# A fixed order for weight sums, loads and roundings at the turn into a two-layer MLP on one core

## The chip, the cores and the metric

The kernel runs on one core of one Trainium2 chip. The metric is device time in microseconds (us). Before the change the median of three runs is 742.66 us (740.46 to 743.09).

A core has five instruction queues that run beside each other and wait for one another through semaphores: TensorE (PE, matrix products), VectorE (DVE), ScalarE (ACT), GpSimd (POOL) and SyncE (SP, which here only issues transfers). Each executes its own instructions in the order in which the program lists them. [...]

## The reference

One block of a language model on 512 tokens with 1024 features, all in float32: an RMS norm, one wide projection, a gated linear attention branch and a softmax attention branch that are merged, an output projection with a residual, and then the part that the change touches.

```python
h = h + merged @ w_out[l]                                          # 1024 x 1024
m = rmsnorm(h, g_mlp[l])
h = h + jnp.square(jax.nn.relu(m @ w_ff1[l])) @ w_ff2[l]           # 1024 x 4096, 4096 x 1024
return rmsnorm(h, g_final)
```

## The kernel before

**Precision.** TensorE multiplies a rounded format (fp32r). To keep float32 accuracy every operand is kept as a rounded part `h` (high, one ScalarE copy that rounds) and a remainder `l` (low, one VectorE subtraction of the rounded part from the original), and each product is three matmuls (`mm3`, lines 88 to 90): high x high, high x low, low x high.

**Seven products instead of eight.** The output projection and each quarter of the MLP cut their operands into 2 x 2 blocks and form the result from seven block products, after Strassen and Winograd. They are numbered 1 to 7. Some of them need a sum of weight blocks. Blocks are called B11, B12, B21, B22; each lies in two tiles, the halves g = 0 and g = 1, of 128 x 1024 numbers (512 KB).

**Phases.** `Mlp(n)` is one phase. There are four quarters; a quarter has a first phase (f0, f1, f2, f3: `m @ w_ff1`) and a second one (g0 to g3: `@ w_ff2`). A first phase runs its products in the order 1, 2, 5, 6, 7, 4, 3. In f0 product 1 reads the weight block in tile B11 as loaded, product 2 reads B21, product 5 reads B11 after **sum 1** (B12 added from memory), product 6 reads B11 after **sum 2** (B22 added as well), product 4 reads B11 after **sum 4** (B21 added), product 7 reads B12 after **sum 3** (B22 added), and product 3 reads B22. So tile B11 goes through a fixed sequence: round (`hi`, line 1616), remainder (`lo`, line 1620), add the next block (`sum`, line 1626), round again. In f0 and in all second phases a sum is an accumulating transfer on GpSimd's queue; in f1 to f3 it is a VectorE addition (line 1628). `load` (line 1606) issues a plain transfer on SP. A second phase keeps its B11 in the tile that w_out's B21 and its last sum used, its B21 where the first phase had B21, and its B12 in the first phase's B12 tile.

**The tokens' side.** `flipped(i)` transposes 128 token rows on TensorE; rows 0 and 1 feed one half of the token blocks, rows 2 and 3 the other. `m_copy` (line 1503) copies the flipped blocks out of the accumulators with the norm's gain, `m_sum` (line 1521) forms sums of token blocks, `m_hi` (line 1508) and `m_lo` (line 1512) round and subtract. `sink` takes a product out of the accumulators.

**The turn.** Before f0 stands the output projection, whose products 1, 2, 5, 6, 3, 7, 4 are traced one by one with everything between them. Rows get their norm as soon as they are complete: `first_half_square` and `second_half_square` (line 174) sum squares on ScalarE, `row_rstd` (lines 181 and 184) makes the row factor on VectorE and GpSimd, `scaled` (lines 1479 and 1480) or, for rows 2 and 3, the last loop of the turn (line 1865) multiplies the row by it.

**What sets the order.** From `begun` on, which is before the output projection's second product, TensorE, ScalarE and VectorE keep the order in which the program is traced (`in_program_order`), and GpSimd keeps it too. The turn is written out statement by statement. After it, every instruction of f0 to g3 is a step with a due time in a table, in units of 10 ns; the steps are sorted by these times and traced in that order. f0 has its own table, `F0_PLACES`; a quarter starts at `base = FLIPS + q * PERIOD`, a first-phase product takes 16 x 36 units and a second-phase product 8 x 22.77 x 3. The times give the order only: an instruction runs as soon as its engine has reached it and its semaphores are there. SP's transfers have no such chain of order of their own.

In the turn as it stands, in f0's order of work: sum 3 is issued after the roundings for w_out's product 4, then come the roundings of f0's B11 and sum 1, the squares and the token copies; product 5's weights are rounded from the step table (540 and 640), after product 2's (340 and 440).

Of the kernel before, what the change touches and what calls it, by code (L numbers as in the profile page):

```python
# [22 lines left out]
KD = D // P  # L23
# [33 lines left out]
def tile_block(ctx: ExitStack, tc: tile.TileContext, t, out: bass.AP):  # L57
# [122 lines left out]
    def row_rstd(parts):  # L180
        nc.vector.scalar_tensor_tensor(
            parts[:, 3:4], parts[:, 1:2], 1.0 / D, parts[:, 2:3], op0=ALU.mult, op1=ALU.add
        )
        nc.gpsimd.tensor_tensor(parts[:, 3:4], parts[:, 3:4], mhalf, op=ALU.pow)
        return parts[:, 3:4]
# [746 lines left out]
    NP = 4  # L932
# [419 lines left out]
    def wo_product(m, rbs=range(2), ps_=range(NP)):  # L1352
        accs = wo_accs.get(m) or wo_accs[1]
        for p in ps_:
            lh, ll = wo_left[p][m]
            wh, wl = wo_right[m][p // 2]
            for rb in rbs:
                tok = slice(rb * P, (rb + 1) * P)
                mm3(accs[rb], lh[:, tok], ll[:, tok], wh[:, p % 2, :], wl[:, p % 2, :],
                    m in (1, 2, 5) and p == 0, p == NP - 1, m not in (1, 2, 5))  # L1360
# [102 lines left out]
    def add_rows(i, c, acc, op=ALU.add):  # L1463
        hc = hrow[i][:, c * S : (c + 1) * S]
        nc.vector.tensor_tensor(hc, hc, acc, op=op)  # L1465
# [8 lines left out]
    def second_half_square(i, c):  # L1474
        square_half(hrow[i], c, hparts[i], ms_rows[i], False)

    def scaled(i, rs):
        m = ms_rows[i]
        nc.vector.tensor_scalar(m[:, 0:S], hrow[i][:, 0:S], rs, None, op0=ALU.mult)
        nc.scalar.activation(m[:, S:D], hrow[i][:, S:D], AF.Copy, scale=rs)  # L1480
# [13 lines left out]
    def m_copy(x, half, ks, by_vector=False):  # L1494
        if x not in m_raw:
            m_raw[x] = pair_tiles(f"mr{x}")
        for k in ks:
            src, gain = fm.block(half, k)
            dst = m_raw[x][k % NP // 2][:, k % 2]
            if by_vector:  # L1500
                nc.vector.tensor_scalar(dst, src, gain, None, op0=ALU.mult)
            else:
                nc.scalar.activation(dst, src, AF.Copy, scale=gain)

    def m_hi(m, b):
        if m not in m_left:
            m_left[m] = quarter(f"mh{m}"), quarter(f"ml{m}")
        nc.scalar.activation(m_left[m][0][:, 2 * b : 2 * b + 2], m_raw[m][b], AF.Copy)
# [72 lines left out]
    class Mlp:  # L1581
# [27 lines left out]
            return self.tiles(self.RIGHT.get(m, B11))  # L1609

        def hi(self, m, g):
            if (self.n, m) == (0, 5):
                self.right[m, g] = [u4(f"{self.name}{m}{g}{x}") for x in "hl"]
            else:
                self.right[m, g] = halves(2, S, f"{self.name}{m}{g}")
            nc.scalar.activation(self.right[m, g][0], self.tile_of(m)[g], AF.Copy)
# [205 lines left out]
    for rb in range(2):  # L1822
        wo_product(3, (rb,))
        add_rows(rb, 1, zs_[rb])
        second_half_square(rb, 1)
        scaled(rb, row_rstd(hparts[rb]))
    wo_product(7, (0,))
    add_rows(2, 1, xs_[0], ALU.subtract)
    wo_right[4] = [split_part(B21, 0, "bo4")]
    wo_right[4].append(split_part(B21, 1, "bo4"))  # L1830
    phases[1].load(B11)
    for g in range(2):
        f0.sum(3, g)
    flipped(0)
    for g in range(2):
        f0.hi(1, g)
    f0.lo(1, 0)
    f0.sum(1, 0)
    first_half_square(2, 1)
    wo_product(7, (1,), range(2))  # L1840
    flipped(1)
    wo_product(7, (1,), range(2, NP))
    add_rows(3, 1, xs_[1], ALU.subtract)
    f0.lo(1, 1)
    f0.sum(1, 1)
    m_copy(1, 0, range(NP))
    for b in range(2):
        m_hi(1, b)
        m_lo(1, b)
    first_half_square(3, 1)  # L1850
    m_copy(2, 0, range(NP, KD))
    for b in range(2):
        m_hi(2, b)
    wo_product(4, (0,))
    add_rows(2, 0, xs_[0])
    wo_product(4, (1,))
    add_rows(3, 0, xs_[1])
    for b in range(2):
        m_lo(2, b)
    second_half_square(2, 0)  # L1860
    rs2 = row_rstd(hparts[2])
    second_half_square(3, 0)
    rs3 = row_rstd(hparts[3])
    for i, r in ((2, rs2), (3, rs3)):
        nc.vector.tensor_scalar(ms_rows[i], hrow[i], r, None, op0=ALU.mult)
    FIRST, SECOND, PERIOD = 36, 22.77, 7857

    steps = []

    def step(at, what, *args):  # L1870
        steps.append((at, len(steps), what, args))
# [17 lines left out]
    for at, ks in ((800, range(2)), (801, range(2, NP))):  # L1889
# [3 lines left out]
    step_pairs(0, {5: (1060, 1115), 6: (1460, 1515), 7: (2055, 2110), 4: (2550, 2600), 3: (3345, 3400)}, m_hi)  # L1893
    step_pairs(0, {5: (1165, 1230), 6: (1540, 1600), 7: (2150, 2260), 4: (2610, 2670), 3: (3480, 3540)}, m_lo)
    F0_PLACES = {
# [6 lines left out]
            4: PLACES["F sink"][4], 3: PLACES["F sink"][3],  # L1902
        },
        "G load": {B21: (1800, 1900), B12: (2240, 2350), B22: (3380, 3500)},
    }
    for m in (4, 3):
        F0_PLACES["F sink"][m] = tuple(x + FLIPS for x in F0_PLACES["F sink"][m])
    for q in range(NQ):
        base, f, g = FLIPS + q * PERIOD, phases[2 * q], phases[2 * q + 1]
        for name, ph in (("F", f), ("G", g)):  # L1910
            at = base
            for m in ph.order:
                if ph.last and m == 4:
                    break
                step_product(at + (7 * slot if ph.second else 0) - (FLIPS if ph is f0 and m == 1 else 0), ph, m)
                at += 8 * SECOND * 3 if ph.second else slot
            for kind in ("hi", "lo", "sum", "load", "sink"):
                kind_of = f"{name} {kind}"
                if q == 0 and kind_of in F0_PLACES:
                    step_pairs(0, F0_PLACES[kind_of], getattr(ph, kind))  # L1920
                    continue
                places = PLACES[kind_of]
                if ph.last and kind == "sink":
                    places = {m: at for m, at in places.items() if m != 4}
                step_pairs(base, places, getattr(ph, kind))
        for kind in ("relu", "square", "left sum", "left hi", "left lo"):
            step_pairs(base, PLACES[kind], getattr(f, kind.replace(" ", "_")))
# [4 lines left out]
        step(base + (7000, 7001, 7250, 7450)[i], out_first, i)  # L1932
    for i in range(2):
        step(base + 7080 + i, out_square, i, slice(0, S))
        step(base + 7180 + i, out_rstd, i)
        step(base + 7440 + 2 * i, out_left, i)
        step(base + 7300 + i, out_right, i)
        step(base + 7441 + 2 * i, out_store, i)
    for _, _, what, args in sorted(steps, key=lambda x: x[:2]):
        what(*args)  # L1940
    in_program_order(begun, PE_ONLY + SPLITTERS)
    in_program_order(attending, (mybir.EngineType.Pool,))
    last_rows(g3)

# [27 lines left out]
```

## Time and profile before

| what | us |
|---|---|
| median of three runs | 742.66 |
| the three runs | 743.09, 742.66, 740.46 |
| the profiled execution, its own time | 743.55 |
| its span | 741.9 |
| TensorE busy | 728.0 (98%) |
| VectorE busy | 626.1 (84%) |
| ScalarE busy | 494.2 (67%) |
| GpSimd busy | 219.4 (30%) |

All times in the views below are from the start of the span of that one execution. A busy TensorE is not a TensorE at its peak: its matmuls are pipelined, and how fast it goes is read from the starts of its matmuls. A name such as `f0x<-mh,f060h` reads: into accumulator f0x, from the tokens' rounded part and from the rounded part of f0's product 6, half 0. `w<-in_w_ff` is a transfer of MLP weights into one of the block tiles: on SP a load, on POOL a sum. In the chain of waits each line is a start, a length and what ran or was waited for. A view of stretches gives the stretch, its length, and for each engine its busy time and number of instructions, then the granted TensorE clock as a share, the busy share of the transfer engines and GB/s. In the list of waits the numbers are the sum, how often, and the longest.

### The profile page before, as it was taken

The page shows a single profiled execution, that of the slowest core. Times are in us where ns is not written, and L with a number is a line of the kernel's source. Part 1 is how long each engine was busy: PE and PEld are TensorE (multiplying, and loading weights), DVE is VectorE, ACT ScalarE, POOL GpSimd, SP SyncE. Part 2 cuts the span into 40 slices and gives each one's busy share as a digit, 9 for nine tenths or more (in the row PEclk, how much of TensorE's full clock was granted, in tenths as well). Part 3 has the DMA queues.
Part 4 walks back from the last instruction along what each step waited for, and adds up shares of the span by engine and source line. Part 5 has one row for each costly group of instructions (what it writes and reads, how often), then busy time and mean ns, then how long its engine had stood idle before and what let it go on. Part 6 is the DMA issues. An engine that isn't in the chain of part 4 may idle for free.

```text
span 741.9 us, 11474 instructions
## 1 busy us (share of the span) xinstructions
PE 728.0 (98%) x4226; PEld 643.0 (87%) x4226; DVE 626.1 (84%) x861; ACT 494.2 (67%) x809; POOL 219.4 (30%) x284
## 2 busy tenths in 40 slices
PE   9999999999999999999999999999999999999995
PEld 7888888888888888899888988889988998899984
DVE  7777887889998788798898879998699869987896
ACT  7557575586596675888856869544774477537764
POOL 0732020242754633146752312200211012101215
PEclk9999999999999999999999999999999999999998
DMA  9849682521221333458988979751987088816763
GB/s 312 270 108 215 215 178 86 89 55 28 64 57 53 50 83 97 111 130 215 270 163 229 229 153 216 191 153 59 245 183 196 15 239 180 196 53 149 167 111 114
DMA packets 80520, 109.95 MB, mean 148 GB/s; under 512 B 15920, under 2 KB 34352, under 8 KB 80464
## 3 DMA queue, kind: packets, MB, share of 16 engines
q1 hardware_dynamic: 63088, 75.64, 32.5%
q0 software_dynamic: 17088, 33.30, 26.6%
q8 instruction: 33, 0.54, 0.3%
q10 hardware_dynamic: 288, 0.28, 0.1%
q14 instruction: 23, 0.19, 0.1%
HBM read 104.22 MB, written 2.10 MB: 143 GB/s over the span
## 4 chain that ended last, share of the span: by engine, by line
PE 84%; DVE 6%; DMA 4%; issue 3%; POOL 1%; ACT 1%; POOLq 0%; DVEq 0%; ACTq 0%
DMA w<-in_w_ff 4%; PE first L326 3%; PE tp L1122 2%; PE zb L88 1%; PE zb L90 1%; PE zb L89 1%; DVE h L1465 1%; PE f1x L89 1%; PE f3x L90 1%; PE f1x L90 1%; PE f2x L90 1%; PE f2x L89 1%; PE f3x L89 1%; PE f3x L88 1%; PE f2x L88 1%
## 5 line engine op out<-in xcount | busy, mean ns | idle before, releaser
L1626 POOL DMA_DIRECT2D w<-in_w_ff x40 | 48.3, 1219 | 260.4 <-DMA w<-in_w_ff 137.1
L1102 DVE TENSOR_REDUCE top<-s 128x1 f32<-128x512 f32 x32 | 21.6, 682 | 4.9 <-PE s L90 4.8
L1107 ACT ACTIVATE e<-s,top 128x512 f32<-128x512 f32 x32 | 22.0, 687 | 3.5 <-DVE top L1102 2.5
L94 DVE TENSOR_TENSOR pT<-tp,pT 128x512 fp32r<-128x512 f32 x32 | 21.8, 683 | 2.4 <-ACT pT L93 1.9
L93 ACT ACTIVATE pT<-tp 128x512 fp32r<-128x512 f32 x32 | 19.1, 596 | 3.2 <-PE tp L1122 3.2
L1122 PE MATMUL tp<-ident,e 128*128 128x128 f32 x128 | 19.5, 274 | 0.0
L88 PE MATMUL av<-pT,v 128*128 128x256 f32 x64 | 19.1, 299 | 0.0
L90 PE MATMUL av<-pT,v 128*128 128x256 f32 x64 | 18.2, 285 | 0.0
L89 PE MATMUL av<-pT,v 128*128 128x256 f32 x64 | 18.1, 284 | 0.0
L1122 PEld LDWEIGHTS tp<-ident,e 128*128 128x128 f32 x128 | 15.2, 140 | 3.1 <-ACT e L1113 0.7
L94 POOL TENSOR_TENSOR qF<-qk,qF 128x512 fp32r<-128x512 f32 x4 | 6.6, 1642 | 37.6 <-ACT qF L93 37.6
L667 POOL DMA_DIRECT2D gvw<-in_w_in x4 | 4.8, 1230 | 38.7 <-DVE gvw L672 34.0
L667 POOL DMA_DIRECT2D zaw<-in_w_in x4 | 4.9, 1228 | 32.7 <-DVE zaw L672 28.0
L1628 DVE TENSOR_TENSOR w<-w,w 128x1024 f32<-128x1024 f32 x12 | 14.4, 1220 | 0.1
L980 POOL DMA_DIRECT2D w<-in_w_out x10 | 12.2, 1400 | 6.5 <-DVE bo60l L94 5.3
L88 PE MATMUL s<-kbuf,q 96*128 96x512 f32 x32 | 14.1, 439 | 0.0
L1153 POOL TENSOR_TENSOR mx<-tb,yg 128x256 f32<-128x256 f32 x8 | 7.7, 964 | 19.8 <-DVE tb L1150 13.9
L577 ACT ACTIVATE bds<-bd 128x512 f32<-128x512 f32 x4 | 2.4, 597 | 15.8 <-PE bd L555 15.8
L89 PE MATMUL s<-kbuf,q 96*128 96x512 f32 x32 | 12.6, 395 | 0.0
L90 PE MATMUL s<-kbuf,q 96*128 96x512 f32 x32 | 12.6, 393 | 0.0
L1113 ACT ACTIVATE e<-e,tot 128x512 f32<-128x512 f32 x16 | 11.6, 726 | 1.3 <-DVE tot L1112 1.3
L89 PEld LDWEIGHTS av<-pT,v 128*128 128x128 f32 x64 | 12.2, 190 | 0.3
(2155 smaller groups left out, 3249.6 us busy)
## 6 DMA issues: line engine op xcount, KB each, us to landing
w<-in_w_ff SPq DMA_DIRECT2D x48, 512.0 KB, 5.5
w<-in_w_ff POOLq DMA_DIRECT2D x40, 512.0 KB, 6.2
w<-in_w_out POOLq DMA_DIRECT2D x10, 512.0 KB, 8.8
grw<-in_w_in SPq DMA_DIRECT2D x8, 512.0 KB, 8.6
zaw<-in_w_in SPq DMA_DIRECT2D x8, 512.0 KB, 7.3
gvw<-in_w_in SPq DMA_DIRECT2D x8, 512.0 KB, 5.0
w<-in_w_out SPq DMA_DIRECT2D x16, 256.0 KB, 5.5
w220f<-in_w_ff SPq DMA_DIRECT2D x8, 512.0 KB, 6.0
```

The lines of the kernel that those rows point to most:

```text
L88: nc.tensor.matmul(acc, lh, rh, start=start, stop=False, skip_group_check=onto)
L89: nc.tensor.matmul(acc, lh, rl, start=False, stop=False, skip_group_check=onto)
L90: nc.tensor.matmul(acc, ll, rh, start=False, stop=stop, skip_group_check=onto)
L93: nc.scalar.activation(hi, src, AF.Copy)
L94: rest.tensor_tensor(lo, src, raw(hi), op=ALU.subtract)
L326: nc.tensor.matmul(f_accs[i], a[:, i * P : (i + 1) * P], b, start=k == 0 and x == 0, stop=k == KD - 1 and x == 2)
L980: nc.gpsimd.dma_start(d, rows.rearrange("(k t p) w -> p t k w", t=2, p=P)[:, x // 2], accum_op=ALU.add)
L1102: nc.vector.tensor_reduce(top, acc, axis=AX.X, op=ALU.max, negate=True)
L1107: nc.scalar.activation(e, acc, AF.Exp, bias=top, accum_out=tot[:, qt % 2 : qt % 2 + 1])
L1122: nc.tensor.transpose(tp[:, k * P : (k + 1) * P], e[:, k * P : (k + 1) * P], ident)
L1626: nc.gpsimd.dma_start(d, self.source(src, g), accum_op=ALU.add)
L1628: nc.vector.tensor_tensor(d, d, self.tiles(src)[g], op=ALU.add)
```

## The change

- The rounding of f0's B11 (`f0.hi(1, ...)`) moves up, between the squares of rows 0 and 1, and with it the remainders and sum 1, ahead of w_out's product 7.
- Sum 3 and the load of g0's B11 leave that place. Sum 3 comes behind sum 2; the load becomes a step (2250 and 2260).
- The rounding, remainder and sum 2 for product 5 move from the step table into the turn, around w_out's product 4, ahead of product 2's rounding, which moves into the turn too. Product 5's rounded weights now lie in the shared `wh`/`wl` buffers, and product 1's in buffers of their own.
- In the step table product 6's second rounding, the remainders and sum 4 get earlier times; the load of g0's B12 and B22 and g0's sum 3 get other times; f1's load of B11 moves from 2802 and 2988 to 6680 and 6690.
- In the last group the row factors of rows 0 and 1 (`out_rstd`) go from 7180 to 7235, which is behind the last weight remainder (7231).
- SP's transfers among the steps are chained in the traced order.

```diff
         def hi(self, m, g):
-            if (self.n, m) == (0, 5):
+            if (self.n, m) == (0, 1):
                 self.right[m, g] = [u4(f"{self.name}{m}{g}{x}") for x in "hl"]
...
         second_half_square(rb, 1)
+        f0.hi(1, rb)
+        if rb == 1:
+            f0.lo(1, 0)
         scaled(rb, row_rstd(hparts[rb]))
+    f0.sum(1, 0)
+    f0.lo(1, 1)
+    f0.sum(1, 1)
     wo_product(7, (0,))
     add_rows(2, 1, xs_[0], ALU.subtract)
     wo_right[4] = [split_part(B21, 0, "bo4")]
     wo_right[4].append(split_part(B21, 1, "bo4"))
-    phases[1].load(B11)
-    for g in range(2):
-        f0.sum(3, g)
     flipped(0)
-    for g in range(2):
-        f0.hi(1, g)
-    f0.lo(1, 0)
-    f0.sum(1, 0)
     first_half_square(2, 1)
...
     add_rows(3, 1, xs_[1], ALU.subtract)
-    f0.lo(1, 1)
-    f0.sum(1, 1)
     m_copy(1, 0, range(NP))
     for b in range(2):
         m_hi(1, b)
         m_lo(1, b)
     first_half_square(3, 1)
-    m_copy(2, 0, range(NP, KD))
-    for b in range(2):
-        m_hi(2, b)
     wo_product(4, (0,))
     add_rows(2, 0, xs_[0])
+    f0.hi(5, 0)
+    f0.lo(5, 0)
+    f0.sum(2, 0)
     wo_product(4, (1,))
     add_rows(3, 0, xs_[1])
-    for b in range(2):
-        m_lo(2, b)
     second_half_square(2, 0)
     rs2 = row_rstd(hparts[2])
     second_half_square(3, 0)
     rs3 = row_rstd(hparts[3])
+    f0.hi(5, 1)
+    f0.lo(5, 1)
+    f0.sum(2, 1)
+    m_copy(2, 0, range(NP, KD))
+    for x in range(2):
+        f0.hi(2, x)
+        m_hi(2, x)
+        f0.sum(3, x)
     for i, r in ((2, rs2), (3, rs3)):
         nc.vector.tensor_scalar(ms_rows[i], hrow[i], r, None, op0=ALU.mult)
+    for x in range(2):
+        f0.lo(2, x)
+        m_lo(2, x)
...
-        "F hi": {2: (340, 440), 5: (540, 640), 6: (1450, 1760), 7: (1985, 2090), 4: (2610, 2710), 3: (3140, 3240)},
-        "F lo": {2: (580, 690), 5: (810, 990), 6: (1640, 1870), 7: (2110, 2225), 4: (2730, 2845), 3: (3250, 3365)},
-        "F sum": {2: (930, 1110), 4: (1760, 1990)},
+        "F hi": {6: (1390, 1520), 7: (1985, 2090), 4: (2610, 2710), 3: (3140, 3240)},
+        "F lo": {6: (1640, 1760), 7: (2110, 2225), 4: (2730, 2845), 3: (3250, 3365)},
+        "F sum": {4: (1650, 1770)},
...
-            1: (1280, 1290), 2: (1310, 1745), 5: (1780, 1975), 6: (2300, 2555), 7: (2860, 3130),
+            1: (1280, 1290), 2: (1310, 1880), 5: (1780, 1975), 6: (2300, 2555), 7: (2860, 3130),
...
-        "G load": {B21: (1800, 1900), B12: (2240, 2350), B22: (3380, 3500)},
+        "G load": {B21: (1800, 1810), B12: (2240, 2270), B11: (2250, 2260), B22: (3400, 3510)},
+        "G sum": {**PLACES["G sum"], 3: (3000, 3100)},
...
+    for m in (1, 2, 4):
+        F0_PLACES["G sum"][m] = tuple(x + FLIPS for x in F0_PLACES["G sum"][m])
...
+                if q == 1 and kind_of == "F load":
+                    places = {**places, B11: (6680 - base, 6690 - base)}
...
-        step(base + 7180 + i, out_rstd, i)
+        step(base + 7235 + i, out_rstd, i)
...
+    stepped = traced()
     for _, _, what, args in sorted(steps, key=lambda x: x[:2]):
         what(*args)
     in_program_order(begun, PE_ONLY + SPLITTERS)
+    in_program_order(stepped, SP_ONLY)
     in_program_order(attending, (mybir.EngineType.Pool,))
```

## The prediction

> **What bounds the kernel now.** I read the page first, then the chain of waits, and then cut the turn into the MLP into stretches, one product of the first group (f0) after another. The page has TensorE busy 98% of the span, so the time can only fall where TensorE stands still, and only the turn and the last microseconds offer that. The view of busy time by stretches, cut where the first matmul of a product starts (product 1, the two late flips, then products 2, 5, 6, 7, 4, 3; columns: stretch, length, then busy time and count of TensorE, its weight loads, VectorE, ScalarE, GpSimd):
>
> ```profile
> 412.13:417.89 5.76, 5.76 (x50) 5.75 (x49) 4.55 (x9) 5.28 (x12) 1.37 (x3) 1.00 1.07 247
> 417.89:419.55 1.66, 1.66 (x18) 1.66 (x17) 1.66 (x3) 0.90 (x1) 0.00 (x0) 1.00 1.16 210
> 419.55:425.38 5.83, 5.83 (x51) 5.83 (x50) 3.64 (x5) 4.53 (x11) 1.38 (x2) 1.00 0.87 234
> 425.38:431.76 6.38, 6.08 (x50) 5.86 (x49) 4.42 (x8) 4.12 (x7) 1.06 (x1) 1.00 0.72 119
> 431.76:439.46 7.70, 6.26 (x51) 5.85 (x49) 7.70 (x10) 6.56 (x11) 2.41 (x2) 1.00 0.59 86
> 439.46:447.18 7.72, 5.92 (x51) 5.75 (x49) 4.23 (x6) 4.29 (x7) 2.03 (x2) 1.00 0.92 262
> 447.18:453.01 5.83, 5.83 (x49) 5.83 (x50) 5.65 (x8) 5.83 (x10) 0.41 (x1) 1.00 0.99 206
> 453.01:458.77 5.76, 5.76 (x51) 5.76 (x50) 4.68 (x7) 5.40 (x9) 1.20 (x1) 1.00 1.04 276
> ```
>
> Seven products do the same work. The undisturbed ones take 5.76, and the flips 1.66. So the group needs 7 x 5.76 + 1.66 = 41.98 us and takes 46.64: **4.66 us are stall**, 0.62 in product 5, 1.94 in product 6, and 1.96 at the end of product 7, where product 4 should begin; 0.14 lies in the rest. The granted clock is 1.00 in every stretch. The chain of waits says who is late (start, length, what):
>
> ```profile
> 407.41 1.23 DVE f010l L1620
> ...
> 408.93 7.56 DMA w<-in_w_ff
> ...
> 420.98 7.75 DMA w<-in_w_ff
> ...
> 428.75 1.06 ACT f060h L1616
> ...
> 435.14 8.89 DMA w<-in_w_ff
> ...
> 444.12 1.07 ACT f041h L1616
> ...
> 447.18 0.36 PE f0x L88
> ```
>
> This is a ladder: a remainder frees block B11, an accumulating transfer adds the next block onto it (sum 1, then sum 2, then sum 4), the result is rounded for products 5, 6, 4, and its remainder lets the next sum start. ScalarE's waits between 398 and 460 us show two of the late rungs:
>
> ```profile
> ACT f041h L1616 <- DMA w<-in_w_ff: 2.4, 1, 2.4
> ACT f060h L1616 <- DMA w<-in_w_ff: 1.8, 1, 1.8
> ```
>
> **The change part by part.** It starts the ladder earlier and puts the rung for product 5 before product 2's operands. No arithmetic is added. I follow the engines' written order from 399 us. Rows that I use (timeline: start, length):
>
> ```profile
> 399.04 0.63 ACT L174 ACTIVATE ms<-h 128x512 f32<-128x512 f32 x1 [3.86 <-DVE h L1465]
> 406.90 1.04 ACT L1616 ACTIVATE f011h<-w 128x1024 fp32r<-128x1024 f32 x1
> 401.12 0.68 DVE L1465 TENSOR_TENSOR h<-h,woz 128x512 f32<-128x512 f32 x1
> 402.59 0.16 DVE L181 SCALAR_TENSOR_TENSOR hp<-hp 128x1 f32<-128x1 f32 x1 [0.79 <-ACT ms L174]
> 405.13 1.23 DVE L94 TENSOR_TENSOR bo40l<-w,bo40h 128x1024 fp32r<-128x1024 f32 x1 [0.62 <-ACT bo40h L93]
> 411.76 1.28 DVE L1465 TENSOR_TENSOR h<-h,wox 128x512 f32<-128x512 f32 x2
> 413.66 1.29 DVE L1512 TENSOR_TENSOR ml<-mr,mh 128x512 fp32r<-128x512 f32 x2 [0.61 <-ACT mh L1508]
> 415.70 1.58 DVE L1865 TENSOR_SCALAR ms<-h,hp 128x1024 f32<-128x1024 f32 x2
> 403.35 2.47 POOL L1626 DMA_DIRECT2D w<-in_w_ff x2
> 406.82 0.39 PE L89 MATMUL wox<-bo40l,gdo 128*128 128x512 f32 x1
> ```
>
> *Sum 1.* The first rounding of B11 moves into ScalarE's idle time at 399.7 and 402.5 (1.04 each, by f011h). The first remainder runs on VectorE at 401.72 (1.23, after the addition at 401.12) to 402.94. It delays the row factor of 402.59 by 0.27, and the scaling behind it to 404.1. The second remainder is done at 405.3. So GpSimd, which issued its first sum at 403.35 after that row factor, issues sum 1 at 403.65 and 405.4 (its two halves), the first instead of 408.93. Price on the path: the additions and the remainders bo40l and bo41l come behind the second remainder, bo40l ends at 407.07 instead of 406.36, and TensorE wants it at 406.82: **+0.3 us**. Bounds: 0 if VectorE's queue closes up better, 0.7 if every step comes as late as bo40l.
>
> *How long a sum takes.* The first fence line is the one sum issued in 403 to 404 us, the second all twelve sums of 400 to 460 us, the third four of a later group without other loads around:
>
> ```profile
> w<-in_w_ff POOLq DMA_DIRECT2D x1, 512.0 KB, 6.0
> ...
> DMA to landing us min/median/max: 5.9/7.5/9.9
> ...
> DMA to landing us min/median/max: 5.8/5.9/6.3
> ```
>
> After the change sum 3 and the load of the second product's B11, four transfers in all, no longer fly beside it. I take 6.2 for the first half (landed at 409.9) and 7.5 for the second (412.9); bounds 5.8 and 9.9.
>
> *Product 5's rounding ahead.* ScalarE reaches it at about 410.0, no wait: rounded at 411.15, remainder at 412.4, sum 2 issued at 412.5. Behind it stand, on ScalarE, the squares of rows 2 and 3; on GpSimd, the powers of their row factors, behind the 1.2 us issue. The addition of row 3 waits for w_out's product 4 (412.4 plus latency) and ends at 413.4, its square at 414.1; then the second rounding ends at 415.1, its remainder at 416.4; sum 2's second half goes out at 416.45. The scaling of rows 2 and 3 (1.58) ends at 417.9, in time for the flips, which begin when product 1 ends (412.43 + 5.76 = 418.2). VectorE then owes product 2 two remainders of weights and two of tokens, 1.14 + 0.60 twice (a long and a short one, back to back): done at 421.4. Product 2 begins at 419.85 and wants the second token half 7 matmuls later, at 420.7: **+0.75 us**, a stall that is new. Bounds: 0, if the chain of additions and squares runs 0.75 quicker; 4.3, if the first sum lands 3.6 later (9.9 instead of 6.2), because everything named here stands behind that wait in three queues.
>
> *Sums 2 and 4.* Sum 2 lands by 420 and 424 at 7.5 each. Product 6's rounding stands at 425.7, so the landing no longer counts; the remainders are done by 430.9, and product 6 starts at 419.85 + 0.75 + 2 x 5.76 = 432.1: the 1.94 goes, and the 0.62 of product 5 with it. Sum 4 goes out at 429.8 and 431.0 instead of 433.33 and 435.14. Even at 9.9 it lands at 441, its rounding and remainder end at 443.4, and TensorE wants that half at 443.6 + 0.7: the 1.96 goes. Cover left: 0.9 at 9.9, 3.3 at 7.5. Sum 3 follows sum 2 on GpSimd's queue and is wanted by product 7 only, at 437.9.
>
> *Loads and SP's order.* The second product's B11 (g0) moves from behind bo41l, about 407, to behind its B12, whose tile product 7's remainder frees at about 435; its first rounding stands 6.3 us before g0 by the kernel's step table (step 3595 of 4222, 10 ns each), about 449, so 14 us cover the transfer. SP's written order adds no wait: matched with the code, its transfers behind the turn already go out in that order, and the stores that swap places at the end are not the last ones. The next group's B11 moves from this group's end to the four issues that begin here:
>
> ```profile
> 483.21 9.06 SPq L1606 DMA_DIRECT2D w<-in_w_ff  x4
> ...
> 490.27 1.06 ACT L1616 ACTIVATE f110h<-w 128x1024 fp32r<-128x1024 f32 x1 [0.67 <-PE g0x L90]
> ...
> w<-in_w_ff SPq DMA_DIRECT2D x2, 512.0 KB, 5.8
> ```
>
> Two loads took 5.8 (median) here. With four in the queue, as the second and third of them, the two halves land by 1.5 to 2 times that, 8.7 to 11.6 after 483.6: at 492.3 to 495.2, where the rounding stands at 490.3. ScalarE waits 2 to 5 us. Their product begins 38.25 us behind 458.77 (7 x 8 x 68.3 steps), at 497.0, and the second half is wanted 0.7 later; rounding and remainder take 1.04 + 1.23, so a landing up to 495.3 is covered. Taken as 0; 1.5 if it is that much later. All of this shifts with the gain.
>
> *The last group's row factors.* Rows of the end, chain first, then VectorE's timeline:
>
> ```profile
> 727.38 1.29 POOL ms L1716
> 728.67 2.03 POOL hp L1726 x2
> ...
> 735.01 0.55 POOL hp L1726
> ...
> 727.41 2.34 DVE L1620 TENSOR_TENSOR g341l<-w,g341h 128x1024 fp32r<-128x1024 f32 x1
> ```
>
> Moved behind g341l, they let it start 0.24 earlier, and GpSimd's powers cannot start before 729.7 instead of 728.67. But the first of the two now takes until about 730.15 (2.03 for two, where one alone takes 0.55), because g341l runs until 729.75; behind g341l both take 0.55: end 730.8 instead of 730.70. I take +0.1; bounds -0.2 and +1.1 (they keep 2.03).
>
> [...]
>
> **Sum.** -4.66 + 0.3 + 0.75 + 0.1 = -3.5 us. The profiled execution took 743.55 (span 741.9 and 1.65 around it) and would take 740.05. It stands 0.9 above the median of the three runs, 742.66, so I predict 742.66 - 3.5 = **739.2 us**. From 458.77 the chain of waits stays on TensorE until VectorE's run at the end begins, released by TensorE, so what is won arrives:
>
> ```profile
> 691.41 0.54 issue
> ```
>
> **Rivals.**
> 1. *The crowd in front of product 2 costs nothing.* All 4.66 is won, also 0.2 at the end: 737.8. For it: VectorE idles 2.3 us in my working between 410 and 415, so 0.75 may close. Against it: the addition of row 3 hangs on TensorE.
> 2. *Given back later.* VectorE has no idle time in the second product:
>
> ```profile
> 460.00:480.00 20.00, 20.00 (x90) 16.58 (x89) 20.00 (x28) 14.06 (x21) 3.63 (x4) 1.00 0.79 188
> ```
>
> If its backlog and not TensorE sets the pace there, only the cover counts: the 46.64 us hold 36.5 of VectorE's work (the column above), 10.1 idle, of which the new order uses up 3.5. So the full loss needs 6.6 more of waits, which speaks against it. Half of the gain lost gives 740.9, all of it 742.7.
> 3. *ScalarE's new wait replaces the old ones: slower.* One place: the rounding for product 5 in ScalarE's queue, with squares, row factors, scaling and product 2's rounding behind it. Each microsecond that sum 1 lands after 410 costs one; it decides from 413.5 on. The slowest pair of sums, of w_out at 380 us, had this median:
>
> ```profile
> w<-in_w_out POOLq DMA_DIRECT2D x2, 512.0 KB, 10.8
> ```
>
> With 10.8, landed at 414.45, it loses 4.5 and the kernel comes to 743.7; for 746.4 the sum would have to land at 417.2, 13.6 after its issue, beyond these rows. Against it: loads of SP flew beside those, and none flies here.
>
> **How the numbers follow.** My forecast has 0.48 (own range 738.0 to 740.4), rival 1 0.30, rival 2 0.12, rival 3 0.10. A measurement of this kernel can tell about 0.5%, 3.7 us, from no change: the border is 738.95. My forecast's centre lies 0.2 above it; I give it 0.22 below and 0.26 above. So faster 0.22 + 0.30 = 0.52; same 0.26 + 0.12 + 0.02 = 0.40; slower the rest of rival 3, 0.08, for orders that no row shows. Range 737.3 to 742.4: from all stall gone, less half a microsecond of scatter between medians, to nearly all given back; it leaves out rival 3 and a part of rival 2.
>
> **What would show it.** Right: sum 1 issued near 403.7 and landed by 413; no wait of ScalarE for sums 2 and 4; products 5, 6, 7 near 5.8 each; product 2 near 6.5, waiting for a token remainder; the second product's start near 455.2. Wrong: ScalarE waiting before f050h, a wait of TensorE in the second product, or f110h waiting more than 3.

## The result and the profile after

| | before | after |
|---|---|---|
| median, us (9 runs each) | 742.82 | 739.14 |
| lowest to highest, us | 740.46 to 743.29 | 738.82 to 739.87 |
| the profiled execution, its own time | 743.55 | 739.87 |
| its span | 741.9 | 738.2 |

The ratio of the times is 0.9954, with a 95% interval of 0.9944 to 0.9964: 3.7 us faster. The forecast was 739.2. Two executions of the runs below, the profiled one of the first run and one of the run without SP's chain, took 1215 us at a granted clock of 0.56, and the medians, ratios and readings leave them out.

The busy time by stretches of the kernel after, cut as before: product 1, the late flips, then products 2, 5, 6, 7, 4, 3.

```profile
412.28:418.04 5.76, 5.76 (x50) 5.75 (x49) 4.05 (x7) 4.83 (x10) 3.98 (x6) 1.00 0.59 91
418.04:419.70 1.66, 1.66 (x18) 1.66 (x17) 1.66 (x3) 1.27 (x3) 1.66 (x2) 1.00 0.74 90
419.70:426.24 6.54, 6.09 (x51) 5.88 (x50) 5.60 (x9) 5.70 (x13) 0.58 (x1) 1.00 1.05 207
426.24:432.00 5.76, 5.76 (x50) 5.76 (x49) 5.10 (x8) 3.58 (x6) 1.74 (x2) 1.00 0.82 197
432.00:437.76 5.76, 5.76 (x50) 5.76 (x49) 4.45 (x7) 5.06 (x8) 0.65 (x1) 1.00 1.07 172
437.76:444.26 6.50, 5.92 (x50) 5.75 (x49) 4.32 (x6) 4.28 (x7) 1.22 (x1) 1.00 0.99 313
444.26:450.09 5.83, 5.83 (x49) 5.83 (x49) 5.65 (x8) 5.83 (x10) 1.21 (x1) 1.00 0.98 175
450.09:455.85 5.76, 5.76 (x51) 5.76 (x49) 4.68 (x7) 5.40 (x9) 1.20 (x1) 1.00 1.04 237
```

The group takes 43.57 us where it took 46.64. Products 5 and 6 no longer stall. Two stalls are left: 0.7 in product 2, which is new, and 0.74 at the end of product 7, where 1.96 stood. The chain of waits through the turn names what each waits for:

```profile
405.62 1.23 DVE bo40l L94
406.90 0.50 PE wox L89
...
419.44 1.14 DVE f021l L1620
420.57 0.61 DVE ml L1512
421.23 0.39 PE f0w L89
...
430.83 0.61 DVE f0a L1672
431.45 9.67 DMA w<-in_w_ff
441.20 1.07 ACT f041h L1616
442.29 1.23 DVE f041l L1620
443.52 0.61 DVE f0a L1672
444.26 0.36 PE f0x L88
```

Read it upwards. TensorE's first matmul of product 4, at 444.26, waits for VectorE's `f0a` (L1672). That is the sink which takes product 7 out of its accumulator, and product 4 is to be written there. The sink ran at 443.52 only, because the remainder f041l stood ahead of it in VectorE's queue, and that remainder waited for sum 4's second half, 9.67 us on its way. The weights themselves were not what TensorE wanted at that moment. GpSimd's timeline gives the issues of the ladder (sums 1, 1, 2, then 2 with 3 and 3, then 4 and 4):

```profile
403.41 1.23 POOL L1626 DMA_DIRECT2D w<-in_w_ff  x1
405.56 1.20 POOL L1626 DMA_DIRECT2D w<-in_w_ff  x1 [0.92 <-DVE f011l L1620]
...
412.33 1.23 POOL L1626 DMA_DIRECT2D w<-in_w_ff  x1 [2.23 <-DVE f050l L1620]
...
416.44 3.85 POOL L1626 DMA_DIRECT2D w<-in_w_ff  x3 [1.61 <-DVE f051l L1620]
430.23 2.42 POOL L1626 DMA_DIRECT2D w<-in_w_ff  x2 [9.95 <-DVE f060l L1620]
```

Sum 1 leaves 5 us earlier than before, sum 2 some 8 to 9. ScalarE reached product 5's first rounding at 409.71 and did not wait:

```profile
409.71 1.06 ACT L1616 ACTIVATE f050h<-w 128x1024 fp32r<-128x1024 f32 x1
```

Of its listed waits in 398 to 460 us one alone is for a transfer:

```profile
ACT f041h L1616 <- DMA w<-in_w_ff: 1.2, 1, 1.2
```

In the profiled pair the span is shorter by 3.7. From the starts of the products: f0 gives 3.07, w_out's product 4 takes 0.33 more (5.87 for 5.54), the start of that product lies 0.17 earlier, and the part after f0 is shorter by 0.77. Between the start of the second product and the last product of all (the accumulator `ge`) both kernels take 267.9 us; so all of the 0.77 lies behind that, at the very end. The timeline of the kernel after, from there:

```profile
721.31 1.30 POOL L1716 TENSOR_TENSOR ms<-h,gfin 128x512 f32<-128x512 f32 x1
...
722.46 1.23 DVE L1620 TENSOR_TENSOR g340l<-w,g340h 128x1024 fp32r<-128x1024 f32 x1
722.69 1.05 POOL L1715 TENSOR_SCALAR hp<-hp 128x1 f32<-128x1 f32 x1
723.61 1.21 DVE L1620 TENSOR_TENSOR g341l<-w,g341h 128x1024 fp32r<-128x1024 f32 x1
723.82 2.16 POOL L1716 TENSOR_TENSOR ms<-h,gfin 128x512 f32<-128x512 f32 x1
724.75 1.31 DVE L1723 SCALAR_TENSOR_TENSOR hp<-hp 128x1 f32<-128x1 f32 x2
...
726.07 1.08 POOL L1726 TENSOR_TENSOR hp<-hp,mhalf 128x1 f32<-128x1 f32 x2
```

and the three rows of before that go with g341l's 2.34 and GpSimd's 1.29:

```profile
724.87 1.29 POOL L1716 TENSOR_TENSOR ms<-h,gfin 128x512 f32<-128x512 f32 x1
...
725.38 1.87 DVE L1620 TENSOR_TENSOR g340l<-w,g340h 128x1024 fp32r<-128x1024 f32 x1
...
726.25 1.05 POOL L1715 TENSOR_SCALAR hp<-hp 128x1 f32<-128x1 f32 x1
```

Now the two remainders run back to back at 1.23 and 1.21, and GpSimd's multiplication beside them takes 2.16 instead of 1.29.

### The profile page after: what moved, and what is told of

Same layout as the page of the kernel before. It is cut to its first block, busy times and chain, and to the rows that moved or that the text cites. A ratio compares the mean times of both kernels' runs of the same rounds, so it can differ in the third digit from the quotient of the medians.

```text
span 738.2 us, 11475 instructions
## 1 busy us (share of the span) xinstructions
PE 726.8 (98%) x4226; PEld 642.2 (87%) x4226; DVE 625.5 (85%) x861; ACT 494.5 (67%) x809; POOL 220.7 (30%) x284
## 4 chain that ended last, share of the span: by engine, by line
PE 91%; DVE 3%; DMA 2%; issue 1%; POOL 1%; ACT 1%; POOLq 0%; DVEq 0%; ACTq 0%
PE first L326 3%; DMA w<-in_w_ff 2%; PE tp L1122 2%; PE zb L88 1%; PE zb L89 1%; PE zb L90 1%; PE f3x L90 1%; PE f2x L89 1%; PE f1x L90 1%; PE f2x L90 1%; PE f1x L89 1%; PE f3x L89 1%; PE f3x L88 1%; PE f1x L88 1%; PE f2x L88 1%
## 5 line engine op out<-in xcount | busy, mean ns | idle before, releaser
L1113 ACT ACTIVATE e<-e,tot 128x512 f32<-128x512 f32 x16 | 11.6, 726 | 1.3 <-DVE tot L1112 1.3
```

## The experiments

All twelve ran beside the kernel before; each ratio is against it, and each expectation names its own theories. Diffs are against the changed kernel unless it is said otherwise. f0 is the time from the first matmul of its product 1 to the second product's first, in the profiled execution: 46.63 before (the rounded stretches add up to 46.64), 43.57 after.

**The row factors back in their old place.**

```diff
-        step(base + 7235 + i, out_rstd, i)
+        step(base + 7180 + i, out_rstd, i)
```

> The changed kernel with the row factors of rows 0 and 1 of the last group back at 7180, between the two last weight remainders. From the start of g0 to the end of the span the changed kernel takes 282.35 us where the kernel before takes 283.08. [...] Theory B (the last sum only landed sooner by chance): the stretch stays near 282.4 and the time at 739.1; the second remainder is long all the same.

Measured: 739.19 us, ratio 0.9955 [0.9942, 0.9969]. The same as the changed kernel, and theory B's 739.1. Had the order made the 0.73 between the two stretches, the time would have come to 739.9. How long the two remainders took in it, no trace shows.

**Product 5's rung back in the step table.**

```diff
-    f0.hi(5, 0)
-    f0.lo(5, 0)
-    f0.sum(2, 0)
...
-    f0.hi(5, 1)
-    f0.lo(5, 1)
-    f0.sum(2, 1)
...
-        "F hi": {6: (1390, 1520), 7: (1985, 2090), 4: (2610, 2710), 3: (3140, 3240)},
-        "F lo": {6: (1640, 1760), 7: (2110, 2225), 4: (2730, 2845), 3: (3250, 3365)},
-        "F sum": {4: (1650, 1770)},
+        "F hi": {5: (540, 640), 6: (1390, 1520), 7: (1985, 2090), 4: (2610, 2710), 3: (3140, 3240)},
+        "F lo": {5: (810, 990), 6: (1640, 1760), 7: (2110, 2225), 4: (2730, 2845), 3: (3250, 3365)},
+        "F sum": {2: (930, 1110), 4: (1650, 1770)},
```

> The changed kernel with product 5's rounding, remainder and sum 2 back in the step table, at the places of the kernel before (540, 640; 810, 990; 930, 1110); sum 1 stays early. Theory A (the rung for product 5 must stand before product 2's operands, or the ladder is late again): product 2 loses its 0.7 us stall, but sum 2 goes out near 421 and 422 instead of 412.3 and 416.4 and sum 4 one to two us later, so product 6 waits 0.3 to 1 and product 4 about 2 more; the group from product 1 to g0 takes 44.5 to 46 instead of 43.6, the time 740 to 741.5. Theory B (starting sum 1 early is all that counts): the group takes 42.9 and the time falls to 738.4.

Measured: 744.11 us, ratio 1.0022 [1.0013, 1.0031]; f0 47.25. It is slower than the kernel before, and beyond what either theory expected. Product 2 is clean, and product 6 takes 9.99 us. ScalarE's timeline, product 5's rounding and product 6's:

```profile
418.05 1.07 ACT L1616 ACTIVATE f050h<-w 128x1024 fp32r<-128x1024 f32 x1
419.00 1.06 ACT L1616 ACTIVATE f051h<-w 128x1024 fp32r<-128x1024 f32 x1
...
429.91 1.06 ACT L1616 ACTIVATE f060h<-w 128x1024 fp32r<-128x1024 f32 x1 [4.30 <-DMA w<-in_w_ff]
```

Sum 1 had landed by 411.9, as in the changed kernel, but the rounding stood in ScalarE's queue until 418.05, behind the squares, the token copies and product 2's roundings. Sum 2 went out at 421.22 and 423.92, behind sum 3 and the load of the second product's B21, and took 8.6 and 8.4 us. The waits between matmuls make only 2.55 us of the 4.23 by which product 6 is too long (0.61, 1.62 and 0.32; one more, of 0.41, lies just ahead of its first matmul). The rest shows in the column of the granted clock, in stretches of the same execution:

```profile
434.00:435.95 1.95, 1.78 (x12) 1.58 (x13) 1.95 (x3) 1.95 (x4) 1.43 (x2) 1.00 0.00 0
435.95:439.40 3.45, 3.45 (x19) 3.45 (x18) 3.45 (x5) 3.45 (x6) 0.97 (x1) 0.51 0.90 138
439.40:441.50 2.10, 2.10 (x19) 2.10 (x19) 1.57 (x3) 0.08 (x1) 0.00 (x0) 1.00 1.08 202
```

After the stall TensorE's granted clock was 0.51 for 3.4 us; half of that is 1.7, and the waits leave 1.68 (4.23 less 2.55). In the end this cost nothing here: product 4 began at 447.80, when the sink in front of it was done, and that sink stood behind sum 4's second half, which had gone out at 435.71, ahead of the half clock.

**The same, with sum 3 behind sum 2**, so that this kernel and the last one differ in what flies beside sum 2 alone. The diff is against the last one:

```diff
-        f0.sum(3, x)
...
-        "F sum": {2: (930, 1110), 4: (1650, 1770)},
+        "F sum": {2: (930, 1110), 3: (1111, 1112), 4: (1650, 1770)},
```

> As the run with product 5's rounding back in the step table (744.1 us), but sum 3 now goes out behind sum 2, so that nothing issued by GpSimd flies beside it. Theory A (the rung itself is late: product 5's rounding stands behind product 2's in ScalarE's queue, near 418, so sum 2 cannot leave before 421): still slower than the changed kernel by 2 to 4 us, 741 to 743.5, with a wait of ScalarE for sum 2's first half of 2 to 3 us and product 6 near 8 us. Theory B (sum 3 in the air ahead of sum 2 is what cost the 5 us there): 739 to 740, product 6 within 0.5 of 5.76.

Measured: 742.22 us, ratio 1.0002 [0.9992, 1.0012]; f0 45.87. Theory A holds in the time: all that the change gained is gone. Sum 3 ahead cost the run above a further 0.002 of 742, 1.5 us. In the trace the place is another one than expected. ScalarE waited 1.4 us for sum 2's first half and product 6 took 6.03; the stall is one rung further, 2.0 in front of product 4, and there the granted clock falls to 0.51 again. Stretches of this execution, from that stall on:

```profile
443.00:445.20 2.20, 0.43 (x3) 0.46 (x4) 2.20 (x4) 1.35 (x4) 0.63 (x1) 1.00 1.11 354
445.20:448.70 3.50, 3.50 (x19) 3.50 (x18) 3.32 (x6) 3.50 (x6) 1.21 (x1) 0.51 0.75 138
448.70:452.10 3.40, 3.40 (x31) 3.40 (x30) 2.16 (x3) 2.33 (x5) 0.00 (x0) 1.00 0.93 195
```

In this execution the half clock makes 1.5 of the 2.3 by which f0 is longer than in the kernel after. The seven executions with a mean clock of 0.996 or more took 740.87 to 742.79, so they lost about as much; where, no trace shows.

**Less traffic, the ladder as before.** On the kernel before: sum 3 leaves the turn and goes behind sum 2, and the load of the second product's B11 becomes a step.

```diff
-    phases[1].load(B11)
-    for g in range(2):
-        f0.sum(3, g)
...
-        "F sum": {2: (930, 1110), 4: (1760, 1990)},
+        "F sum": {2: (930, 1110), 3: (1111, 1112), 4: (1760, 1990)},
...
-        "G load": {B21: (1800, 1900), B12: (2240, 2350), B22: (3380, 3500)},
+        "G load": {B21: (1800, 1900), B11: (2250, 2260), B12: (2240, 2350), B22: (3380, 3500)},
```

> The kernel before with sum 3 (now behind sum 2, steps 1111 and 1112) and the load of g0's B11 (step 2250) taken out of the turn; nothing else moves. Theory A (the order of the ladder counts, not the traffic): sum 1 lands in about 6 us instead of 8.8, but the next rung waits for VectorE's remainders all the same, sum 2 still goes out near 421 and sum 4 near 433 and 435; the 4.66 us of stall fall by at most 1.2, the time to 741.5 to 742.5. Theory B (the crowded transfers were the cause): sum 2 goes out 2.5 us earlier, the stalls fall by 2.5 or more, the time to 740.2 or less.

Measured: 742.79 us, ratio 1.0008 [0.9997, 1.0019]; f0 45.95. No gain. The edit did only half of what it was to do: SP's transfers are not chained in this kernel, and its trace still shows the load leaving at 406.03 and 407.17. Only sum 3 is gone. Sum 1's halves landed after 7.1 and 8.5 us (8.8 and 9.7 before), yet sum 2's first half left at 420.63, when it left before (420.98; the turn lies 0.35 earlier in this execution). Product 5's remainder stood as far back in VectorE's queue, behind product 2's two, which ran from 416.84 to 419.11. Sum 2's second half went out 1 us earlier against the products, and f0 is 0.7 shorter in this execution, but the median shows no gain.

**The traffic back, the ladder as changed.** The other corner: sum 3 and that load fly beside sum 1 again.

```diff
+    phases[1].load(B11)
+    for g in range(2):
+        f0.sum(3, g)
     flipped(0)
...
-        f0.sum(3, x)
...
-        "G load": {B21: (1800, 1810), B12: (2240, 2270), B11: (2250, 2260), B22: (3400, 3510)},
+        "G load": {B21: (1800, 1810), B12: (2240, 2270), B22: (3400, 3510)},
```

> The changed kernel with sum 3 and the load of the second product's B11 back in the turn, in front of the late flips, so that both fly beside sum 1 again; the ladder's order stays. Theory A (the order of the ladder is what gained): sum 1 lands up to 3 us later (first half near 410, second near 415), product 5's second rounding waits for it by 0 to 1, and the kernel stays within 1 us of the changed one, 739 to 740.2. Theory B (the lighter traffic is a part of the gain): sum 1 takes 9 us as before the change, product 2's operands stand behind the waiting rounding, product 2 takes over 8 us, and the kernel comes to 741 to 743.

Measured: 739.35 us, ratio 0.9959 [0.9945, 0.9972]; f0 42.77. The whole gain is there, as theory A has it. Sum 1's halves took 5.8 and 8.1 us, and sum 2's took (issues between 411.9 and 416.2, median to landing):

```profile
w<-in_w_ff POOLq DMA_DIRECT2D x2, 512.0 KB, 11.7
```

Twice the 5.9 of the later group's sums, which had no other loads around, and the rounding for product 6 waited 0.4 us in all. The ladder now starts so early that it bears the crowd.

**Only the load of the second product's B11 back in the turn.**

```diff
+    phases[1].load(B11)
     flipped(0)
...
-        "G load": {B21: (1800, 1810), B12: (2240, 2270), B11: (2250, 2260), B22: (3400, 3510)},
+        "G load": {B21: (1800, 1810), B12: (2240, 2270), B22: (3400, 3510)},
```

> The changed kernel with the load of g0's B11 back in the turn, behind the remainders for w_out's product 4 (near 407). Theory A: sum 1's second half, then in flight, lands near 413.5 instead of 412.0, still before ScalarE asks for it (413.8); sum 4's second half has two loads less beside it near 435 and lands about 1 us earlier than 441.1, so the 0.74 us stall before product 4 shrinks to 0 to 0.3; time 738.4 to 739.0. Theory B (the load collides with sum 1): ScalarE waits for sum 1 by 1 us or more, product 2 starts or runs that much later, time 740 or more.

Measured: 739.38 us, ratio 0.9962 [0.9946, 0.9977]; f0 42.94. The median lies between the two theories, and no loss against the changed kernel is shown. Sum 1's second half landed at 414.37, product 5's second rounding came 0.2 later for it, and product 2 took 6.72, 0.18 more than in the kernel after. The stall before product 4 is gone, as theory A has it.

**SP's transfers not chained.**

```diff
-    in_program_order(stepped, SP_ONLY)
```

> The changed kernel without the chain of order on SP's transfers. Theory A (the chain costs and gains nothing): the same time within 0.3 us, 739.1, and SP's issues behind the turn in the same order except the stores at the end. Theory B (the order holds a load back that would otherwise start early and collide): some load starts at another time and the time moves by 0.5 us or more.

Measured: 739.04 us, ratio 0.996 [0.9945, 0.9975]; f0 42.76. The chain is worth nothing here. Without it SP issued a pair of loads at 406.81 and 407.94 by itself, beside sum 1, as in the run above.

**Product 7's first sink ahead of product 4's second remainder.**

```diff
-        "F lo": {6: (1640, 1760), 7: (2110, 2225), 4: (2730, 2845), 3: (3250, 3365)},
+        "F lo": {6: (1640, 1760), 7: (2110, 2225), 4: (2730, 2861), 3: (3250, 3365)},
```

> The changed kernel with one number changed: the remainder of product 4's second weight half goes from 2845 to 2861, behind the first sink of product 7 (2860) in VectorE's queue. Theory A (the 0.74 us stall before product 4 is the accumulator, not the weight: the sink stands behind a remainder that waits for sum 4): the stall goes, product 7's stretch is 5.8 instead of 6.5, the time falls by 0.7 to 0.8 us to 738.4. Theory B (the weights of product 4 are late themselves): the stall moves inside product 4 and the time stays at 739.1.

Measured: 739.11 us, ratio 0.9955 [0.9943, 0.9967]; product 7's stretch 5.76, f0 42.75. The stall is gone, but it is also gone in the three runs just above, which leave the sink where it was: there, and in this run too (8.3), sum 4's second half landed 8.2 to 8.5 us after its issue, and not 9.67. So the stall comes and goes with that landing, and the edit's worth in the median is not shown.

**Product 2's first weight half rounded early.**

```diff
     second_half_square(2, 0)
+    f0.hi(2, 0)
     rs2 = row_rstd(hparts[2])
+    f0.lo(2, 0)
...
-        f0.hi(2, x)
+        if x:
+            f0.hi(2, x)
...
-        f0.lo(2, x)
+        if x:
+            f0.lo(2, x)
```

> The changed kernel with the rounding of product 2's first weight half moved up into ScalarE's gap (411.4 to 413.2) and its remainder into VectorE's gap behind the row factor of row 2 (413.2). Theory A (product 2's stall of 0.7 us is VectorE's queue, four remainders behind the scaling): the second token remainder ends near 420.4 instead of 421.2, the stall goes or falls below 0.1, the time falls by 0.7 us to 738.4. Theory B (the row factors and the scaling come so much later that the flips or product 2 wait instead): the gain is under 0.3 us.

Measured: 738.63 us, ratio 0.9948 [0.9935, 0.9962]; f0 42.05. Its stretches, product 2 and product 5:

```profile
419.99:425.81 5.82, 5.82 (x51) 5.82 (x50) 3.74 (x7) 5.58 (x13) 0.58 (x1) 1.00 1.07 201
425.81:431.57 5.76, 5.76 (x50) 5.76 (x49) 5.66 (x8) 3.77 (x6) 1.59 (x2) 1.00 0.74 151
```

Product 2's stall of 0.72 is gone, so it was the crowd of remainders behind the early rung. The median is 0.5 lower, though the intervals overlap.

**Both of the last two.**

> The changed kernel with both edits: product 2's first weight half rounded in ScalarE's gap, and the remainder of product 4's second half behind product 7's first sink. If the two stalls are independent, as the theory has it, both gains add: the group from product 1 to g0 takes 42.1 instead of 43.6, the time falls by 1.4 us to 737.7. If removing one only makes the next transfer late (sum 4 is asked for 0.7 us earlier), the gain is 0.7 to 0.9 us: 738.3.

Measured: 738.48 us, ratio 0.9952 [0.9939, 0.9966]; f0 42.05, which is the 41.98 without stalls but for 0.07. It is the lowest median of all, 0.15 below the one before it, which these runs cannot tell apart. The expected 737.7 for two gains that add did not come. In the run before it the stall before product 4 was gone already, so the sink's place had nothing left to win there.

**Both, and f0's second remainder behind w_out's first.** What is left is the 0.3 us in w_out's product 4, where TensorE waits for bo40l. The diff is against the run with both:

```diff
-    f0.lo(1, 1)
-    f0.sum(1, 1)
     wo_product(7, (0,))
...
     wo_right[4] = [split_part(B21, 0, "bo4")]
+    f0.lo(1, 1)
+    f0.sum(1, 1)
```

> The version with product 2's first weight half rounded early and product 7's sink ahead of the waiting remainder (738.48 us), and besides the second remainder of f0's B11 behind the first remainder of w_out's B21. Theory A: TensorE no longer waits for that remainder, 0.3 us, and sum 1's second half leaves 1.2 to 2 us later without a wait at product 5's second rounding: 738.1 to 738.3, w_out's product 4 at 5.54. Rival: sum 1's second half lands near 414.5, product 5's second rounding waits, and product 2 takes 0.5 to 1.5 more: 738.7 to 740.

Measured: 739.19 us, ratio 0.9955 [0.9943, 0.9967]. Both theories fail on the place. Product 5's rounding did not wait, and product 2 is clean, but w_out's product 4 takes 6.35. TensorE's waits:

```profile
PE wox L89 <- DVE bo41l L94: 0.6, 1, 0.6
```

The remainder put in front of bo41l made that one late instead, and TensorE waited 0.74 us between matmuls for it, where bo40l cost 0.25.

**The row factors alone.** On the kernel before, with nothing else changed:

```diff
-        step(base + 7180 + i, out_rstd, i)
+        step(base + 7235 + i, out_rstd, i)
```

> The kernel before with the later row factors of the last group as its only edit. Theory A (worth about 0.13 us, read from the end of the run against the last rounding): 0.9998 of the kernel before, within its interval. Theory B (worth the 0.77 by which the profiled ends differ): 0.9990, at or below the lower end of the interval around 1. Either way the last two weight remainders run back to back at about 1.22 each.

Measured: 742.42 us, ratio 1.0003 [0.9994, 1.0012]. No gain is shown; 0.9990 is outside the interval. Its end looks like that of the kernel after:

```profile
723.88 1.31 POOL L1716 TENSOR_TENSOR ms<-h,gfin 128x512 f32<-128x512 f32 x1
724.99 1.28 DVE L1620 TENSOR_TENSOR g340l<-w,g340h 128x1024 fp32r<-128x1024 f32 x1
726.19 1.21 DVE L1620 TENSOR_TENSOR g341l<-w,g341h 128x1024 fp32r<-128x1024 f32 x1
...
726.40 2.16 POOL L1716 TENSOR_TENSOR ms<-h,gfin 128x512 f32<-128x512 f32 x1
```

## Why the prediction was right, step by step

**The stalls of products 5 and 6 (-0.62, -1.94): right, and for the reason given.** The order of the ladder gains, not the lighter traffic. Of four corners the kernel before is one (ratio 1); with sum 3 taken out of the crowd alone it is 1.0008, with the new order alone and the crowd back 0.9959, with both 0.9954. (Where sum 3 alone was taken out, the load of B11 still flew; that load alone, put back into the changed kernel, lost nothing that the median shows.) Sum 1's earlier start is not enough either. With product 5's rung back in the table it lands as early as after the change, and the gain is gone (1.0002). What counts is that the rung, the rounding in ScalarE's queue and the remainder in VectorE's, stands where the sum lands. The two moved together in every run, so their shares are not told apart. The earlier table times of product 6's second rounding, its remainders and sum 4 stayed in both runs without the gain, so they do not make it alone; whether it needs them was not tried.

**Sum 1 and product 5's rounding: right.** Issues at 403.41 and 405.56 (predicted 403.65 and 405.4), 5.98 and 6.39 us to landing (6.2 and 7.5), the rounding at 409.71 without a wait (410.0), sum 2 at 412.33 and 416.44 (412.5 and 416.45).

**w_out's product 4, +0.3: right,** 0.33, of which the wait for bo40l that was named is 0.25.

**Product 2, +0.75: right,** 0.72, by the token remainder that was named, and taken away by the run that rounds a weight half earlier.

**Product 4, -1.96: the step that failed in part.** It said "Even at 9.9 it lands at 441, its rounding and remainder end at 443.4, and TensorE wants that half at 443.6 + 0.7". Sum 4 landed at 441.12 after 9.67, and the remainder was done at 443.5, both as worked out. But 0.74 us of stall stayed in the profiled execution. I had asked when TensorE wants the weights. It wanted the accumulator first, and the sink that frees it stood behind that remainder. I had followed the chain of waits to ScalarE's f041h and from there straight to TensorE, one link short of the sink. TensorE's list of waits before the change had named it:

```profile
PE f0x L88 <- DVE f0a L1672: 1.8, 1, 1.8
```

The cover was not 0.9 us at that landing but below nothing. In four other runs with the early rung and the sink in its old place (the crowd back, B11's load back, no chain on SP, product 2's half early) the half landed earlier and the stall was not there, so the term is between -1.2 and -1.96. Two of the signs that the prediction named for being right failed with it in the profiled execution: ScalarE waited 1.2 for sum 4, and product 7's stretch is 6.50 instead of 5.8. None of its signs for being wrong came.

**The loads, 0: right.** TensorE has no wait in the second product. f110h waits 2.5 us, inside the 2 to 5 foreseen, though the four loads took 6.0 to 7.7 us and not 8.7 to 11.6. The second product's B11 may fly early or late, to no effect on the median in three runs.

**The end, +0.1: mis-sized, and the sign wrong.** The profiled ends differ by -0.77, but only 0.12 of it is the order. From ScalarE's rounding of g341h to the end the old order takes 19.01 and 19.03 us (two traces), the new one 18.87 to 18.92 (ten traces, the row factors alone among them; an eleventh, whose last sum took 7.42, has 18.14). GpSimd's queue sets this end. The two powers that I priced end 5.84 us after its multiplication at 721.31; before, 5.82 after 724.87: +0.02, where I had +0.1. What I left out is GpSimd's work behind them, up to the end of the power at 731.32, which takes 4.72 now and took 4.87: there the last power but one waited 0.29 for VectorE, and now it does not. So VectorE's two remainders, which now end 1.2 us sooner against the end, win only 0.13, because GpSimd's multiplication beside them takes 0.87 longer, 2.16 for 1.29. The other 0.65 is the landing of the last sum of all, the row of before and the row of after:

```profile
w<-in_w_ff POOLq DMA_DIRECT2D x1, 512.0 KB, 6.3
```

```profile
w<-in_w_ff POOLq DMA_DIRECT2D x1, 512.0 KB, 5.7
```

It is scatter as far as the runs show: with the old turn and only the row factors moved it took 5.74, and in the run with product 5's rung back 7.42.

**The sum.** -3.5 was predicted and -3.68 measured, in the medians and in the profiled pair alike. In that pair two errors cancel: f0 gave 0.84 less than the 3.91 of its terms (4.66 less 0.75), and the end 0.87 more than its +0.1. In the run without SP's chain, where the stall before product 4 is away, f0 gives 3.87; with +0.33 and -0.12 that is -3.66. So the medians agree without the two accidents.

**The rivals.** Rival 1 (the crowd costs nothing) did not come here, since product 2's stall did. The version with a weight half rounded early has f0 without stalls, and comes to 738.63 where the rival put 737.8. Rival 2 (given back later) is out: from the second product to the last the time is 267.9 in both. Rival 3 (ScalarE's new wait) did not come: sum 1's first half landed at 409.4, in the other runs with the early rung at 410.1 at the latest, and the second as late as 414.46 without a wait (in another run 414.37, at a cost of 0.18). What a later one would cost was not tried.

## What to carry to other kernels

Where one buffer is refilled again and again, put each rounding into its engine's queue at the place where the refill lands, and let the next refill's start be the reason for the order; lighter traffic around it was worth little here once the chain had slack (0.9959 with the crowd back, 0.9954 without). When you cost a late operand, follow the chain one link past it: what stands behind the waiting instruction on its engine may be wanted sooner than the operand itself, as the sink was here. And before you price two engines whose instructions take longer beside each other, as the remainder's 2.34 us for 1.21 and the multiplication's 2.16 for 1.29 here, find out which of their queues sets the end.

## What the runs showed of the hardware that was not expected

**A stall can be followed by half a clock.** In both traces where product 5's rung came late after an early sum 1, TensorE's clock fell to a half for 3.4 us behind a stall (0.51 in the stretches from 435.95 and from 445.20, 1.00 on both sides). The second time it cost 1.5 us (7.32 in product 4, where the kernel after has 5.83); the first time product 4 waited anyhow. The second time a stall of 2.1 us between two matmuls' starts, 1.8 of it idle, stood ahead of it. It isn't for certain, though: the runs with less traffic and with the row factors alone kept the full clock (1.00) with 1.7 and 1.5 us ahead of product 4, and the kernel before with the same 2.1:

```profile
445.00:447.20 2.20, 0.40 (x5) 0.23 (x3) 1.99 (x3) 1.35 (x4) 1.98 (x2) 1.00 0.64 202
447.20:450.60 3.40, 3.40 (x28) 3.40 (x29) 3.22 (x5) 3.40 (x6) 0.39 (x1) 1.00 0.94 158
```

A half clock for 3.4 of 740 us lowers an execution's mean by 0.002, worked out from the 0.51. The mean is 0.996 to 0.998 mostly. It is 0.995 or less in 9 of 11 executions of the run with product 5's rung back, in 3 of 10 with sum 3 behind it, in 6 of the 51 of the kernel before that ran beside the experiments, and in 1 of the 46 of the changed kernel and its variants with the early rung (0.995). That those six of before had the same episode, no trace shows. Nor do the times show its cost plainly: with the rung back, the two executions with a mean of 0.996 and 0.997 took 744.49 and 744.11, as long as the others. Why the half clock followed such a stall in one execution and not in another, no run here tests.

**Sums beside other transfers took longer.** A 512 KB sum took 5.7 us at the end of the kernel after, and 11.7 us (the median of sum 2's halves) in the run where sum 3 and the load of B11 were back in the turn. The last of three sums in a row, sum 3's second half, landed 13.75 us after its issue in the turn of the kernel after.
